# An encoder trunk on one core: attention units spread through the mixer, the Fourier parts reordered, and the second product of a gate block moved

## The chip, the core and the metric

One core of a Trainium2 chip runs the whole program: two layers of a bidirectional encoder on 512 tokens of width 1024, all in 32-bit floats. The metric is the time of one execution on the device in microseconds (us), as the median of several runs. Besides that there is one execution taken by the hardware profiler, with a record of every instruction; all rows of the profile are from it.

The engines have short names in the rows: PE is TensorE (matmuls), DVE is VectorE, ACT is ScalarE, POOL is GpSimd, SP is SyncE, which here only issues DMAs.

## The reference

Each of the two layers does three steps, and a norm stands at the end:

```python
x = x + 0.5 * swiglu(rms_norm(x, ffn1_norm[l]), ffn1_w_in[l], ffn1_w_out[l])
x = x + mixer(rms_norm(x, mix_norm[l]), mix_w_in[l], mix_gate_bias[l], na_rpb[l],
              na_w_out[l], f_w_out[l], mix_w_o[l])
x = x + 0.5 * swiglu(rms_norm(x, ffn2_norm[l]), ffn2_w_in[l], ffn2_w_out[l])
```

The change touches only the mixer. From one projection of the normed input it takes q, k, v (8 heads of 64), u (512 columns) and two gate inputs (1024 columns each):

```python
y_na = neighbourhood_attention(q.reshape(shp), k.reshape(shp), v.reshape(shp), rpb) @ w_na_out
y_f = fourier_mix(uf) @ w_f_out
g_na = jax.nn.sigmoid(ga + gate_bias[0])
g_f = jax.nn.sigmoid(gf + gate_bias[1])
return (g_na * y_na + g_f * y_f) @ w_o
```

The attention is local: on a grid of 8 x 64 tokens each query sees 8 x 16 keys, with a learned bias per head and offset, and a softmax over them. The Fourier part is the real part of a two-dimensional DFT over positions and over the 128 channels of each of four groups.

## The kernel before, in words

**Split matmuls.** Every 32-bit operand that goes through a matmul is cut into a high half, which the fast matmul type holds exactly, and a low half, the rest. A product is three matmuls: high x high, high x low, low x high. For weights this is `Item.prep` (line 192): ACT makes `whi` (L206; L201 with a minus sign; L186 in `prep_high`), DVE makes `wlo` (L209, L202, L190). Where the weight is a sum or difference, DVE first adds a second block in place (L178). There are three buffers each for `whi` and `wlo`.

**The stream of weights.** The weights come as blocks ("granules") of 128 x 1024, 512 KB, in one list that `stage_items` writes out in the order of use. `Stream.fetch` issues loads on SP's queue up to `FETCH` = 8 items ahead of the last prepared one, but never beyond the current stage; `Stream.enter` opens the next stage. Some blocks are sums that a DMA makes: POOL issues a load that adds to what is there (L164, and L211, which turns the weight of product 6 into that of product 3). `Stream.next(ahead)` prepares the item that is due and `ahead` (mostly 2) more.

**Products by Strassen.** A large product of 2 x 2 blocks is made from seven smaller ones, numbered 1 to 7 (`product`, lines 551 to 577). Each takes two granules and, with both halves of 256 tokens, 24 matmuls. The weights of the seven come from the quadrants a, b, c, d: product 1 takes -a, 2 takes b, 4 takes d (loaded anew), 5 takes d - c, 6 takes that plus a, 7 takes c - a and 3 takes product 6's weight with b added by POOL (signs lie in the sums). So b is a plain load, while product 5's weight is a load and a DMA that adds onto it. `ORDER` = (1, 5, 2, 6, 7, 3, 4) is the order in the gates.

**The mixer before the change** (`stage_mixer`), in order:

1. `proj_UV`: u and v by seven products, with projections of q and k (`proj_T`, one head pair each) between them.
2. Fourier transform over positions (`four_pos`, `rotated`) and over channels (`four_ch`, `four_mid`, `four_high`, `four_ends`).
3. Attention in eight units of `Probs` (two per head pair): scores on PE (`att_scores`, L1397), maxes with the bias on DVE (L1413), exps on ACT (L1422), reciprocals of the sums (L1425), scaling on ACT (L1430), transposes on PE (`transposed`, L1438), a copy by ACT (`kept`, L1448), then per head pair the product with v (`att_pv`, L1463) and the split of its result (`att_split`, L1473 and L1474). The units went in pairs: 0 and 1, 2 and 3, and so on, each pair's steps close together.
4. The Fourier output's product with its weights, in an even part (`part_f` with m = 0, plus the ends) and an odd part (m = 1) per half i of the output columns and per half t of the tokens. `f_copy` takes the even part, `f_both` makes their sum and difference, `f_last` adds single rows by short DMAs of POOL (L1671, L1673), `f_turn` puts the sums in their mirrored places by eight DMAs of SP (L1661) for each i. Order before: even 0, odd 0, even 1, odd 1, strewn between the attention units.
5. `swap_pools(0)`: the mixer's own pool of tiles is closed, its memory becomes nine buffers for weights, and the gates' stage opens. This stands behind the transposes of units 6 and 7.
6. `fill`: the attention output's product with its weights (L337 to L339), left half of the columns.
7. Two gate blocks (`gate_block`) of seven products each, whose results go through tanh and multiply the two outputs (`arg`, `with_f`, `with_n`). In block 1 the outputs of block 0 are turned over by transposing DMAs (`apart`, L374, and `joined_words`, L387). Then the rest of the attention output's product and the product with w_o.

**What sets the order.** From the start of `proj_UV` to the last `f_turn`, PE, DVE and ACT run in the order in which the program is written (the `manual_schedule` blocks). The queues of SP and POOL aren't written out by hand: a planner puts their DMAs in place, in about the program's order, and a queue runs strictly in its order, so that a DMA that waits holds those behind it. The gate blocks themselves are planned for PE and DVE too, with parts of ACT in written order.

Of the kernel before, what the change touches and what calls it, by code (L numbers as in the profile page):

```python
# [23 lines left out]
TB = T // P  # L24
# [8 lines left out]
ORDER = (1, 5, 2, 6, 7, 3, 4)  # L33
FETCH = 8
# [63 lines left out]
def encoder_kernel(  # L98
# [117 lines left out]
    def stage_items():  # L216
# [52 lines left out]
        for l in range(L):  # L269
# [16 lines left out]
            for i in range(2):  # L286
                strassen(s, lambda q: "g" + q, i, two, ORDER, True)
# [834 lines left out]
    def stage_mixer(l, norm, nxt):  # L1122
# [74 lines left out]
        vt, vch = [None] * TB, {}  # L1197
# [18 lines left out]
        def proj_UV():  # L1216
# [30 lines left out]
            step(6)  # L1247
            q0 = proj_T(DH**-0.5)
# [32 lines left out]
            product(pa, acts[7], K4, False, again=True, ahead=0)  # L1281
            ws.depth = FETCH
# [83 lines left out]
        o, q, k, bms = [], {}, {}, {}  # L1366
# [136 lines left out]
        def gate_block(i, bias, acts, after):  # L1503
# [37 lines left out]
            for m in ORDER:  # L1541
# [52 lines left out]
        yf = []  # L1594
# [80 lines left out]
        first_f = []  # L1675
        with tc.manual_schedule(engines={mybir.EngineType.DVE, mybir.EngineType.Activation}):
            with tc.manual_schedule(engines={mybir.EngineType.PE}):
                u, k1, pa, sb, acts4 = proj_UV()
                fp = [four_pos(0), four_pos(1)]
                bias_for(0)  # L1680
                k1 = k1()
                ws.prep(ws.pos + 2)
                bt = [rotated(fp[0]), rotated(fp[1])]
                less(pa, sb)
                k[1] = k1()
                ends_load()
                q2 = proj_T(DH**-0.5)
                q2 = q2()
                p0, p1 = [Probs(i, att_scores(i)) for i in range(2)]
                p0.maxes(0)  # L1690
                p0.maxes(1)
                ws.prep(ws.pos + 3)
                p0.exps(0)
                p1.maxes(0)
                p0.inverse(0)
                p0.exps(1)
                p1.maxes(1)
                p0.inverse(1)
                p1.exps(0)
                product(pa, acts4, K4, False, again=True, ahead=0)  # L1700
                q[2] = q2()
                for c in range(2):
                    value(c, pa[c])
                f0 = four_ch(bt)
                bias_for(1)
                p1.exps(1)
                fp = [four_pos(2), four_pos(3)]
                p1.inverse(0)
                p1.inverse(1)
                k2 = proj_T(None, 0)  # L1710
                for c in range(2):
                    value(2 + c, sb[:, c, :])
# [3 lines left out]
                p0.scaled(0)  # L1716
                y0 = y0()
                p0.scaled(1)
                bt.append(rotated(fp[1]))
                p1.scaled(0)  # L1720
                p1.scaled(1)
                k2 = k2()
                ws.prep(ws.pos + 2)
                key_rows()
# [5 lines left out]
                q3 = proj_T(DH**-0.5, 0, hook=second)  # L1730
                y1 = four_high(fq[0], 1)
                ye = four_ends(fq[1])
                q3 = q3(False)
                yf += [y0, y1()]
                ye()
                ends_split()
                ts = transposed(p0.s) + transposed(p1.s)
                pt_ = {0: kept(ts[0:2]), 1: kept(ts[2:4])}
                q3 = q3()
                p2, p3 = [Probs(i, att_scores(i)) for i in (2, 3)]  # L1740
                k3 = proj_T(None, 0)
                p2.maxes(0)
                p2.maxes(1)
                ws.prep(ws.pos + 1)
                low = ws.prep_high()
                p2.exps(0)
                p2.exps(1)
                p2.inverse(0)
                p3.maxes(0)
                p2.inverse(1)  # L1750
                low()
                p2.scaled(0)
                p2.scaled(1)
                p3.exps(0)
                p3.maxes(1)
                k[2] = k2()
                p3.inverse(0)
                p3.exps(1)
                q[3] = q3()
                p3.inverse(1)  # L1760
                p3.scaled(0)
                p3.scaled(1)
                k3 = k3(False)
                bias_for(2)
                first_f.append(ws.next(0))
                raw = ws.items[ws.pos - 1].raw.t
                first_f.append(ws.next(0))
                pf = part_f(0, 0, first_f[0], 0)
                ts = transposed(p2.s)
                f_copy(0, 0, pf)  # L1770
                pf = part_f(0, 1, first_f[0], 0)
                pl = last_f(0, raw)
                pt_[2] = kept(ts)
                k3 = k3()
                ts = transposed(p3.s)
                f_copy(0, 1, pf)
                pt_[3] = kept(ts)
                f_last(0, pl)
                k[3] = k3()
                p4, p5 = [Probs(i, att_scores(i)) for i in (4, 5)]  # L1780
                po = [att_pv(0), att_pv(1)]
                p4.maxes(0)
                p4.maxes(1)
                ws.prep(ws.pos + 1)
                p4.exps(0)
                p5.maxes(0)
                p4.inverse(0)
                p4.exps(1)
                p5.maxes(1)
                p4.inverse(1)  # L1790
                p4.scaled(0)
                p4.scaled(1)
                bias_for(3)
                ws.enter(ws.stage + 1)
# [81 lines left out]
        for _ in fill(o, ns, 0, w):  # L1876
            pass
# [324 lines left out]
```

## Time and profile before

| | |
|---|---|
| median of 3 runs | 1876.02 us |
| the three runs | 1877.15, 1876.02, 1864.79 us |
| profiled execution, its own time | 1877.13 us |
| span of its instructions | 1875.3 us |
| mean granted clock of PE | 0.993 |
| PE busy | 1834.1 us, 98% |
| DVE busy | 1604.9 us, 86% |
| ACT busy | 1305.6 us, 70% |
| DMA | 405.87 MB, mean 216 GB/s |

A row of groups reads: line, engine, operation, out <- in by the program's names, shapes, count | busy us, mean ns of one | idle time just before them and what ended it. A row of a timeline reads: start us, length us, engine, line, operation, out <- in, count, and in brackets the idle time before it with what ended it. A row of waits reads: who <- whom: total us, times, longest. A row of stretches reads: from:to, length, then for each engine the busy time and the number of instructions, the granted clock (1.00 is full), the busy share of the DMA engines (it can come out a little over 1) and GB/s. Records of matmuls overlap, since they are pipelined, so the pace of a run of matmuls is read from their starts. "SPq" is SP's queue issuing a DMA.

### The profile page before, as it was taken

How to read it: one execution, taken by the hardware profiler on the slowest of the kernel's cores; microseconds unless marked ns; L12 is line 12 of the kernel's file. 1: busy time of each engine (PE TensorE's matmuls, PEld its weight loads, DVE VectorE, ACT ScalarE, POOL GpSimd, SP SyncE). 2: the span in 40 equal slices, each digit the busy share in tenths (PEclk: the TensorE clock that was granted, in tenths of full speed). 3: DMA queues.
4: the chain of work that ended last, by engine and by line, in shares of the span. 5: the costliest groups of instructions: out<-in, count | busy, mean ns of one | idle time of the engine just before them, and what ended most of it. 6: DMA issues, size and time to landing. Idle time of an engine off the chain costs nothing.

```text
span 1875.3 us, 24536 instructions
## 1 busy us (share of the span) xinstructions
PE 1834.1 (98%) x8778; PEld 1513.5 (81%) x8778; DVE 1604.9 (86%) x1938; ACT 1305.6 (70%) x1775; POOL 187.5 (10%) x231
## 2 busy tenths in 40 slices
PE   9999999999899999999999999999998899999998
PEld 7888888887678888888888888877877688888886
DVE  7878899877789988889998879988778699888899
ACT  6777876657576767786666778665675677677865
POOL 0001010100101011001011000101011100110010
PEclk9999999999999999999999999999999899999999
DMA  9898798863987689879878987978549977998795
GB/s 297 225 237 219 194 266 279 207 180 111 271 219 180 158 236 238 215 208 275 248 188 225 220 219 205 285 264 174 157 148 246 202 181 174 224 229 217 202 286 149
DMA packets 206770, 405.87 MB, mean 216 GB/s; under 512 B 109116, under 2 KB 109276, under 8 KB 206648
## 3 DMA queue, kind: packets, MB, share of 16 engines
q1 hardware_dynamic: 176536, 302.61, 51.0%
q0 software_dynamic: 29680, 101.14, 30.1%
q8 instruction: 69, 1.13, 0.2%
q10 hardware_dynamic: 432, 0.55, 0.1%
q14 instruction: 53, 0.43, 0.1%
HBM read 372.76 MB, written 2.11 MB: 200 GB/s over the span
## 4 chain that ended last, share of the span: by engine, by line
PE 88%; DMA 5%; DVE 4%; ACT 1%; issue 1%; SPq 0%; POOL 0%; DVEq 0%; ACTq 0%; POOLq 0%
PE A L532 9%; PE A L535 9%; PE A L533 9%; PE o L535 6%; PE o L532 6%; PE o L533 6%; PE B L533 5%; PE B L535 5%; PE B L532 5%; DMA raw<-in_wst_dram 3%; PE ps L337 3%; PE ps L338 3%; PE ps L339 3%; PE C L532 2%; PE C L533 2%; PE C L535 2%
## 5 line engine op out<-in xcount | busy, mean ns | idle before, releaser
L209 DVE TENSOR_TENSOR wlo<-raw,whi 128x1024 fp32r<-128x1024 f32 (+1 forms) x532 | 629.8, 1195 | 189.2 <-ACT whi L206 186.7
L206 ACT ACTIVATE whi<-raw 128x1024 fp32r<-128x1024 f32 (+1 forms) x532 | 544.0, 1034 | 292.2 <-DMA raw<-in_wst_dram 59.4
L164 POOL DMA_DIRECT2D raw<-in_wst_dram x170 | 148.8, 895 | 1216.8 <-DMA raw<-in_wst_dram 527.6
L178 DVE TENSOR_TENSOR raw<-raw,raw 128x1024 f32<-128x1024 f32 (+1 forms) x152 | 181.6, 1195 | 2.0
L532 PE MATMUL A<-whi,xh 128*128 128x512 f32 x400 | 155.9, 390 | 2.7 <-ACT whi L201 2.7
L533 PE MATMUL A<-whi,xl 128*128 128x512 f32 x400 | 155.7, 389 | 0.0
L387 ACT ACTIVATE at<-zt 128x1024 uint16<-128x1024 uint16 (+2 forms) x96 | 110.4, 1168 | 12.3 <-DMA zt<-zs 12.1
L201 ACT ACTIVATE whi<-raw 128x1024 fp32r<-128x1024 f32 (+1 forms) x83 | 85.6, 1036 | 45.4 <-PE A L533 13.6
L535 PE MATMUL A<-wlo,xh 128*128 128x512 f32 x400 | 115.0, 389 | 0.0
L202 DVE SCALAR_TENSOR_TENSOR wlo<-raw,whi 128x1024 fp32r<-128x1024 f32 (+1 forms) x83 | 98.6, 1195 | 16.3 <-ACT whi L201 16.3
L532 PEld LDWEIGHTS A<-whi,xh 128*128 128x128 f32 x400 | 75.1, 188 | 18.9 <-ACT whi L201 3.5
L535 PEld LDWEIGHTS A<-wlo,xh 128*128 128x128 f32 x400 | 75.1, 188 | 15.6
L533 PEld LDWEIGHTS A<-whi,xl 128*128 128x128 f32 x400 | 75.1, 188 | 15.4
L533 PE MATMUL C<-whi,xl 128*128 128x512 f32 x208 | 81.0, 389 | 0.0
L533 PE MATMUL B<-whi,xl 128*128 128x512 f32 x208 | 81.0, 389 | 0.0
L532 PE MATMUL B<-whi,xh 128*128 128x512 f32 x208 | 81.0, 389 | 0.0
L532 PE MATMUL C<-whi,xh 128*128 128x512 f32 x208 | 81.0, 389 | 0.0
L368 ACT ACTIVATE zs<-th 128x1024 uint16<-128x1024 uint16 x80 | 79.5, 1042 | 0.9 <-DVE th L792 0.9
L785 ACT ACTIVATE th<-sn,rh 128x512 f32<-128x512 f32 x80 | 54.9, 716 | 32.7 <-DVE sn L622 31.8
L617 ACT ACTIVATE sn<-A 128x512 f32<-128x512 f32 x104 | 58.6, 586 | 25.2 <-PE A L535 25.2
L535 PE MATMUL C<-wlo,xh 128*128 128x512 f32 x208 | 60.1, 390 | 0.0
L535 PE MATMUL B<-wlo,xh 128*128 128x512 f32 x208 | 59.8, 389 | 0.0
(446 smaller groups left out, 4643.3 us busy)
## 6 DMA issues: line engine op xcount, KB each, us to landing
raw<-in_wst_dram SPq DMA_DIRECT2D x472, 512.0 KB
raw<-in_wst_dram POOLq DMA_DIRECT2D x180, 512.0 KB, 8.1
bm<-in_bias_dram SPq DMA_DIRECT2D x16, 512.0 KB
raw<-in_wst_dram SPq DMA_DIRECT2D x30, 256.0 KB
vs<-v SPq DMA_DIRECT2D x24, 128.0 KB
x<-in_xin_dram SPq DMA_DIRECT2D x4, 512.0 KB
raw<-in_wst_dram POOLq DMA_DIRECT2D x8, 256.0 KB, 7.8
dft<-in_dft_dram POOLq DMA_DIRECT2D x8, 256.0 KB, 6.7
```

The costliest lines, as they stand in the source:

```text
L164: G.dma_start(out=self.t, in_=wst[GRAN_AT[self.plus]][:, 0 : self.n], accum_op=ALU.add)
L178: V.tensor_tensor(self.raw.t, self.raw.t, self.add.t, self.op)
L201: S.activation(hi, t, AF.Copy, scale=-1.0)
L202: self.last = V.scalar_tensor_tensor(lo, t, -1.0, hi.bitcast(F32), ALU.mult, ALU.subtract)
L206: S.activation(hi[:, cs], t[:, cs], AF.Copy)
L209: self.last = V.tensor_tensor(lo[:, cs], t[:, cs], hi[:, cs].bitcast(F32), ALU.subtract)
L368: S.activation(s[:, h], words[:, h], AF.Copy)
L387: S.activation(to[:, w], t[:, w], AF.Copy)
L532: PE.matmul(ps, lh, rh, start=start, stop=False, skip_group_check=again)
L533: PE.matmul(ps, ll, rh, start=False, stop=False, skip_group_check=again)
L535: PE.matmul(ps, lh, rl, start=False, stop=stop, skip_group_check=again)
L617: S.activation(t[:, b, :], ps[b], AF.Copy)
```

## The change

Five things, all of them in the order of work; no operation is added or taken away.

- **Scores spread.** `proj_UV` now issues the scores of unit 0 behind the projection of q1 and those of unit 1 behind product 3, with their maxes, exps, reciprocals and part of the scalings among the rest of the u/v work. Units 2 to 7 follow one at a time, each with its own transposes, instead of in pairs. The bias of the first head pair is loaded from within `proj_UV`, the others earlier than before.
- **Even parts first.** The two even Fourier parts of both i (with their weights, which now come first in the stream) are done between units 4 and 7, with `f_last` for both at once. The odd parts come last: i = 0 ahead of the transposes of unit 7, i = 1 behind them.
- **The swap and the row turns.** `swap_pools(0)` stands behind the transposes of unit 7, now the last. Behind it come the odd parts of i = 1, the last `att_pv`, and both `f_turn`, which before stood ahead of it (i = 0) and behind it (i = 1). The attention output's weights are fetched later (`ws.enter` behind the split of `po[2]`).
- **Order at the hand-over.** `fill` is inside the written order for DVE and ACT now, with the first gate weight prepared ahead of it, and the sums of activations t1 to t3 are placed around it.
- **Gates.** Block 0 takes its products in the order `FIRST` = (1, 2, 5, 6, 7, 3, 4), and the stream lists its weights so.

```diff
+FIRST = (1, 2, 5, 6, 7, 3, 4)
...
-            for i in range(2):
-                t1, t2 = (s, "f", 2 * i), (s, "f", 2 * i + 1)
+            halves = [((s, "f", 2 * i), (s, "f", 2 * i + 1)) for i in range(2)]
+            for t1, t2 in halves:
                 add(Raw(t1, plus=t2))
+            for t1, t2 in halves:
                 add(Raw(t1), Raw(t2), op=ALU.subtract)
...
-                strassen(s, lambda q: "g" + q, i, two, ORDER, True)
+                strassen(s, lambda q: "g" + q, i, two, ORDER if i else FIRST, True)
...
             k[0] = k0()
+            p.append(Probs(0, att_scores(0)))
             product(pb, acts[3], K4, False, again=True)
             q1 = q1()
+            p[0].maxes(0)
+            p[0].maxes(1)
+            p[0].exps(0)
+            p[0].exps(1)
+            p.append(Probs(1, att_scores(1)))
             less(pb, s2)
+            p[0].inverse(0)
+            p[0].inverse(1)
...
             constants()
+            p[1].maxes(0)
+            p[1].maxes(1)
+            p[0].scaled(0)
+            p[0].scaled(1)
...
             product(pa, acts[7], K4, False, again=True, ahead=0)
+            ws.prep(ws.pos + 1)
+            p[1].exps(0)
+            p[1].exps(1)
```

The end of the attention, as it is after the change:

```python
                p.append(Probs(7, att_scores(7)))
                p[6].inverse(0)
                p[6].inverse(1)
                f_w.append(ws.next(0))
                raws.append(ws.items[ws.pos - 1].raw.t)
                pf = [part_f(0, t, f_w[1], 1) for t in range(2)]
                pl = [last_f(i, raws[i]) for i in range(2)]
                p[7].maxes(0)
                p[7].maxes(1)
                p[6].scaled(0)
                p[6].scaled(1)
                p[7].exps(0)
                p[7].exps(1)
                f_copy(1, 0, pf[0])
                f_copy(1, 1, pf[1])
                for i in range(2):
                    f_last(i, pl[i])
                po.append(att_pv(2))
                ts = transposed(p[6].s)
                p[7].inverse(0)
                p[7].inverse(1)
                p[7].scaled(0)
                p[7].scaled(1)
                first = minus(B[0, 0], B[0, 1], "t1")
                next(first)
                next(first)
                pt_[6] = kept(ts)
                att_split(po[2])
                ws.enter(ws.stage + 1)
                ws.prep(ws.pos + 2)
                f_w.append(ws.next(0))
                f_both(0, 0, part_f(1, 0, f_w[2]))
                f_both(0, 1, part_f(1, 1, f_w[2]))
                ts = transposed(p[7].s)
                swap_pools(0)
                pt_[7] = kept(ts)
                f_w.append(ws.next(0))
                ws.prep(ws.pos + 2)
                pf = [part_f(1, t, f_w[3]) for t in range(2)]
                po.append(att_pv(3))
                f_both(1, 0, pf[0])
                att_split(po[3])
                f_both(1, 1, pf[1])
                f_turn(0)
                f_turn(1)
                t12, _ = next(first)
                third = minus(B[0, 1], B[1, 1], "t3")
```

And the hand-over to the gates:

```diff
+            w = [ws.next(0), ws.next(0)]
+            ws.prep(ws.pos + 1)
             h1 = high(t12, "t1")
-            ws.prep(ws.pos + 3)
-            third = minus(B[0, 1], B[1, 1], "t3")
-            next(third)
             acts[5] = low(h1, t12, "t1")
+            for _ in fill(o, ns, 0, w):
+                pass
             for z in B[1, 1]:
                 V.tensor_tensor(t12, t12, z, ALU.add)
             h2 = high(t12, "t2")
             next(third)
             acts[6] = low(h2, t12, "t2")
-            w = [ws.next(), ws.next()]
-        for _ in fill(o, ns, 0, w):
-            pass
+            next(third)
...
-        ga0 = gate_block(0, bias, acts, {1: third_parts, 6: fourth})
+        ga0 = gate_block(0, bias, acts, {1: third_parts, 6: fourth}, FIRST)
```

More of the change, by code (lines that the diff above doesn't have):

```diff
@@ L1501, in fill, with gate_block @@
                 yield
-        def gate_block(i, bias, acts, after):
+        def gate_block(i, bias, acts, after, order=ORDER):
             r = norm.r
@@ L1540, in gate_block @@
             ga = [None, None]
-            for m in ORDER:
+            for m in order:
                 if m == 1:
@@ L1763, in stage_mixer @@
+                p[5].exps(0)
+                p[5].exps(1)
                 k3 = k3(False)
[L1764 to L1773, printed above, removed]
@@ L1805, in stage_mixer @@
-                ts = transposed(p4.s) + transposed(p5.s)
-                pt_[4] = kept(ts[0:2])
-                pt_[5] = kept(ts[2:4])
-                second_f = [ws.next(0)]
-                raw = ws.items[ws.pos - 1].raw.t
-                p6, p7 = [Probs(i, att_scores(i)) for i in (6, 7)]
-                po = att_pv(2)
-                p6.maxes(0)
-                ws.prep(ws.pos + 1)
-                p6.maxes(1)
-                p6.exps(0)
-                p7.maxes(0)
-                p6.inverse(0)
@@ L1818, in stage_mixer @@
-                p6.exps(1)
-                p7.maxes(1)
-                p6.inverse(1)
-                p6.scaled(0)
-                p6.scaled(1)
-                pf = [part_f(0, t, second_f[0], 1) for t in range(2)]
-                second_f.append(ws.next(0))
-                pl = last_f(1, raw)
-                f_turn(0)
-                p7.exps(0)
-                p7.exps(1)
+                bias_for(3)
+                f_w = [ws.next(0)]
+                raws = [ws.items[ws.pos - 1].raw.t]
```

174 lines of the change are left out of this document (82 added, 92 removed).

## The prediction

> **What bounds the kernel now.** First the page: TensorE (PE) is busy nearly the whole span, so a gain has to come from its pauses.
>
> ```profile
> span 1875.3 us, 24536 instructions
> PE 1834.1 (98%) x8778; PEld 1513.5 (81%) x8778; DVE 1604.9 (86%) x1938; ACT 1305.6 (70%) x1775; POOL 187.5 (10%) x231
> ```
>
> Then the busy time by stretches (us, PE, PEld, DVE, ACT, POOL, granted clock, DMA share, GB/s), cut where the mixer's parts begin and end; first layer 0, then layer 1.
>
> ```profile
> 367.60:405.00 37.40, 37.40 (x207) 31.20 (x206) 29.16 (x58) 21.46 (x44) 5.00 (x8) 1.00 0.77 229
> 405.00:460.00 55.00, 53.60 (x418) 42.41 (x417) 40.89 (x113) 45.09 (x119) 4.08 (x6) 1.00 0.26 78
> ...
> 470.28:486.75 16.47, 12.08 (x49) 8.70 (x48) 10.49 (x10) 9.34 (x13) 2.30 (x3) 1.00 1.02 290
> 486.75:497.85 11.10, 11.10 (x49) 8.93 (x48) 11.10 (x12) 6.22 (x8) 1.85 (x3) 1.00 0.89 252
> 497.85:509.52 11.67, 7.34 (x26) 5.59 (x24) 7.79 (x9) 4.82 (x6) 1.72 (x2) 0.85 1.05 274
> 509.52:520.40 10.88, 10.88 (x50) 9.01 (x48) 10.88 (x14) 6.27 (x7) 1.73 (x2) 1.00 0.81 207
> 520.40:561.40 41.00, 38.41 (x170) 31.45 (x168) 33.55 (x36) 30.73 (x34) 3.48 (x4) 1.00 0.85 216
> ```
>
> ```profile
> 1334.00:1389.00 55.00, 53.60 (x419) 42.41 (x418) 40.90 (x113) 45.08 (x119) 4.07 (x6) 1.00 0.27 77
> ...
> 1399.43:1415.89 16.46, 12.90 (x50) 9.79 (x48) 9.55 (x9) 9.31 (x13) 1.72 (x2) 0.90 1.02 285
> ...
> 1427.03:1436.81 9.78, 7.36 (x26) 5.57 (x25) 7.99 (x9) 4.83 (x6) 1.72 (x2) 0.83 1.04 269
> ...
> 1447.71:1496.32 48.61, 40.80 (x169) 33.23 (x168) 33.50 (x36) 30.82 (x34) 3.81 (x5) 0.89 0.89 192
> ```
>
> Gate block 0 begins at 470.28. Products 3 and 4 (509.52 to 520.40) run without a pause, so a product costs 10.88 / 2 = 5.44 and one of its 24 matmuls 0.227. Against that, products 1 and 5 lose 16.47 - 10.88 = 5.59 (layer 1: 5.58), product 7 loses 11.67 - 5.44 = 6.23 (layer 1: 9.78 - 5.44 = 4.34). That is **21.74** in all. Block 1 loses 41.00 - 38.08 = 2.92 and 10.53 more. Attention (405 to 460, 1334 to 1389) pauses 1.40 a layer, while the DMA engines stand at 0.26 and 0.27; in the gates they are full.
>
> ```profile
> PE A L532 <- ACT sn L617: 4.3, 1, 4.3
> PE B L532 <- ACT whi L206: 2.5, 2, 1.8
> PE A L532 <- ACT whi L201: 1.8, 1, 1.8
> ```
>
> ```profile
> PE A L532 <- ACT sn L617: 2.4, 1, 2.4
> ```
>
> These are PE's waits in block 0 of layer 0, and the one of product 7 in layer 1. The first is product 7: PE waits for the snapshot of product 6, which ACT holds back behind a weight that hasn't landed:
>
> ```profile
> 478.63 1.06 ACT L206 ACTIVATE whi<-raw 128x1024 fp32r<-128x1024 f32 x1 [1.77 <-DMA raw<-in_wst_dram]
> ...
> 496.69 0.60 ACT L617 ACTIVATE sn<-A 128x512 f32<-128x512 f32 x1 [1.20 <-PE A L535]
> 502.11 1.06 ACT L206 ACTIVATE whi<-raw 128x1024 fp32r<-128x1024 f32 x1 [4.82 <-DMA raw<-in_wst_dram]
> 503.07 0.58 ACT L617 ACTIVATE sn<-A 128x512 f32<-128x512 f32 x1
> ```
>
> The row at 478.63 is the first half of d for product 5, which came 8.4 after the gates' start. The weight at 502.11 is product 3's: quadrant d, to which POOL adds b in place (L211) once product 6's low half is made. POOL's issues, block 0 and block 1, and the page's median landing:
>
> ```profile
> 492.98 0.86 POOL L211 DMA_DIRECT2D raw<-in_wst_dram  x1 [6.09 <-DVE wlo L209]
> ...
> 535.54 0.87 POOL L211 DMA_DIRECT2D raw<-in_wst_dram  x1 [17.75 <-DVE wlo L209]
> ```
>
> ```profile
> raw<-in_wst_dram POOLq DMA_DIRECT2D x180, 512.0 KB, 8.1
> ```
>
> And SP's queue, which says why the gates' weights start late: their first six loads stand behind the row turns L1661, which wait for the last odd part.
>
> ```profile
> 322.52 0.80 SPq L1372 DMA_DIRECT2D bm<-in_bias_dram  x2
> ...
> 402.67 7.61 SPq L1208 DMA_DIRECT2D vs<-v  x12
> ...
> 457.13 4.24 SPq L1661 DMA_DIRECT2D fs<-gs  x5
> 461.49 3.56 SPq L154 DMA_DIRECT2D raw<-in_wst_dram  x6
> ...
> 1386.31 4.24 SPq L1661 DMA_DIRECT2D fs<-gs  x5
> 1390.66 2.96 SPq L154 DMA_DIRECT2D raw<-in_wst_dram  x6
> ```
>
> **The change, part by part.** No matmul, activation or DVE operation is added or removed; all is order. Prices:
>
> ```profile
> L209 DVE TENSOR_TENSOR wlo<-raw,whi 128x1024 fp32r<-128x1024 f32 x504 | 611.4, 1223 | 187.6 <-ACT whi L206 185.1 <-PE o L533 1.4 <-PE A L535 0.8
> ...
> L1413 DVE CUSTOM_DVE_ANT_0 s<-ps,bm 128x256 f32<-128x256 f32 x64 | 23.7, 418 | 0.7 <-PE ps L1397 0.7
> ```
>
> ```profile
> L206 ACT ACTIVATE whi<-raw 128x1024 fp32r<-128x1024 f32 x504 | 526.8, 1056 | 286.5 <-DMA raw<-in_wst_dram 57.6 <-DVE raw L178 57.0 <-PE A L533 54.6
> ...
> L1422 ACT ACTIVATE s<-s,nmx 128x256 f32<-128x256 f32 x64 | 31.6, 498 | 1.3 <-DVE nmx L1413 1.3
> L1430 ACT ACTIVATE s<-s,rs 128x256 f32<-128x256 f32 x64 | 27.0, 501 | 4.3 <-DVE rs L1425 4.2
> ```
>
> ```profile
> L1438 PE MATMUL ps<-ident,s 128*128 128x128 f32 x128 | 16.6, 275 | 1.8 <-ACT s L1430 1.8
> L1463 PE MATMUL ps<-p,vs 128*64 128x128 f32 x256 | 15.3, 275 | 0.0
> ...
> L1642 PE MATMUL ps<-raw,nyq 128*32 128x512 f32 x16 | 4.2, 605 | 0.0
> ```
>
> (1) *Scores spread.* A unit is 12 short score matmuls, four maxes (23.7 / 64 x 4 = 1.5; 1.7 by the mean) on DVE, four exps (2.0) and four scalings (1.7) on ACT. Units 0 and 1 go into 367.6 to 405, where DVE is busy 29.16 and ACT 21.46 of 37.40: 3.4 and 7.4 us fit. The tightest place there is the first Fourier product, which needs the low halves of u:
>
> ```profile
> 379.46 2.50 DVE L1192 TENSOR_TENSOR u<-ue,u 128x512 fp32r<-128x512 f32 x4
> ```
>
> They end at 381.96, PE comes at 367.60 + 3 x 5.44 = 383.92: 2.0 to spare. The eight maxes (3.0 to 3.4) and short reciprocals push them back by 3.4 to 4, the two scores push PE back by some 1.8 with their changes of kind, and the last halves are wanted one to two us into the product. So I count nothing; if that cover is gone, it costs up to 2 a layer. The 1.40 of pauses stand between pairs of units (transposes behind scalings); with one unit at a time each scaling has at least 5 us of PE's other work ahead of it, so 2.8 are gained for both layers (bound: 0). Two more changes of matmul kind per layer cost some 0.2 each: 0.8 (an estimate, 0 to 0.8).
>
> (2) *Even parts first, odd behind.* The last odd parts now need their weights prepared behind unit 7's softmax. From the scores of unit 7 on, PE has two even parts (16 matmuls, 3.7), two last rows (4.2 / 4 each, 2.1), a P·V product (15.3 / 8 = 1.9), two sets of transposes (16.6 / 16 each, 2.1) and two odd parts (2.7): 12.5 us before it wants them. ACT and DVE have to finish unit 6's exps (2.0, and some 2 until they begin), then copies of transposes (1.0), scalings (1.7), exps (2.0), two differences (2.4), the split of a head's output (0.6), the high half (1.0) and the low half (1.2): about 14. So a new wait of 0 to 1.8, for which I take 1.1 a layer: 2.2.
>
> (3) *SP and POOL.* The biases move up (before, SP issued them at 322.52, long ahead of use), the twelve row copies L1208 move behind the values: some 7.6 us from about 407, wanted at about 428: nothing. All 16 row turns move behind the gates' first loads. From the last transposes (where the pool is swapped) PE has 12 matmuls of odd parts (2.7), a P·V product (1.9) and 48 of the fill (10.9) before the gates: 15.5 us. The loads began 470.28 - 461.49 = 8.8 ahead; now up to 15.5. Both short accumulate chains of the last Fourier rows now come just ahead of the swap on POOL; the pool's memory or POOL may hold loads until about where they start now. That is the lower bound of the head start: none.
>
> (4) *Product 2 second.* Quadrant b is a plain load; d needs a load and then an accumulate (8.1). Now d comes 8.4 after the gates' start (478.63) and is wanted at 5.44; after the change it is wanted at 10.9, with b's two loads ahead of it. Even without a head start nearly all of product 5's wait is covered; with it, all. I leave 0.5 a layer for the second half of product 1's weights (0 to 1.8, today's wait L201, since ACT still makes t2's high half about there): 1.0.
>
> (5) *Product 7.* POOL's L211 goes out 0.57 after product 6 begins (497.85 - 5.44 = 492.41). In block 1 product 6 begins at 520.40 + 16.32 = 536.72, so it goes out 1.2 before; without the squeeze that the late d makes, ACT and DVE can do it as soon as product 2's buffers are free, up to 2.9 before. The snapshot is wanted 5.44 + 0.9 = 6.3 after the start; landing 8.1 (page) to 9.1 (492.98 to 502.11) and a high half of 1.0: left over 0 to 2.6. I take 1.3 a layer, 2.6, and no slow clock behind it (0.85 and 0.83 in the two stretches of product 7 now).
>
> [...]
>
> **Sum**: 21.74 - 1.0 - 2.6 + 2.8 - 2.2 - 0.8 = 17.9 off the profiled execution's 1877.13, which is 1.1 above the median of 1876.02: **1858**. Bounds: 21.74 + 2.8 = 24.5 to 21.74 - 3.6 - 5.2 + 2.8 - 3.6 - 0.8 = 11.3, so 1852 to 1865.
>
> **Rivals.** (A) *Block 1's wait goes as well.* In block 1 ACT waits for a transposing DMA:
>
> ```profile
> 1476.52 1.34 ACT L387 ACTIVATE mq<-zt 128x1024 uint16<-128x1024 uint16 x1 [7.61 <-DMA zt<-zs]
> ```
>
> If layer 1 behaves like layer 0, 48.61 becomes 41.00, 7.6 less: **1850**. For it: one of three runs shown is 11 shorter, and earlier weights leave the transposes freer. Against it: the steps around it aren't changed.
>
> (B) *The gates are bound by bytes.* Block 0 moved 290 x 16.47 + 252 x 11.10 + 274 x 11.67 + 207 x 10.88, 13.0 MB; at 290 GB/s that is 44.9 us, not 38.1. Without a head start layer 0 wins 50.12 - 44.9 = 5.2 and layer 1, whose block 0 takes 1447.71 - 1399.43 = 48.28, wins 3.4: **1867**. With 6.7 of head start it just fits. [...]
>
> (C) *It doesn't do what it says*: swap and loads stay where they are, and only product 5's wait shrinks, about 4 a layer: **1868**.
>
> (D) *Slower: the written order blocks.* ACT, DVE and PE run strictly in it, and now a maxes or exps stands ahead of the next weights' split at 16 places. If each holds PE by its four maxes (1.7), that is 27 against 18 gained: **1885**. It decides from 1.1 us a place. Against it: DVE has 8 and ACT 16 us free in the stretch that takes units 0 and 1.
>
> **How the numbers follow.** Forecast 0.50, A 0.20, B 0.17, C 0.05, D 0.08. A measurement of this kernel tells about 1% from no change, here below 1857.3. The forecast's own range lies on both sides of that, a little less than half below (0.24); with nearly all of A, faster 0.43. Slower is D less its small cases, 0.07; the rest, 0.50, is within 1%. The range from 1847 (A with some of the forecast's upside) to 1874 leaves out D and the tails.
>
> **What would show it.** Right: block 0 at 38 to 41 us in both layers, product 5 third and without a wait, six gate loads issued 12 us or more ahead of the first gate product, clock 1.00 in product 7, attention with pauses of at most 2 us. Wrong: waits of PE for whi or wlo of the odd parts or for s at more than two places of 1 us; a DMA share still near 1.0 with PE waiting in product 7 or 3; gate start later than now relative to the u/v product's start.

## The result and the profile after

| | before | after |
|---|---|---|
| median | 1873.95 us (11 runs, 1864.79 to 1877.15) | 1861.78 us (11 runs, 1857.66 to 1869.91) |
| profiled execution | 1877.13 us | 1860.03 us |
| span of its instructions | 1875.3 us | 1858.3 us |

The ratio after to before is **0.9943, 95% interval 0.9924 to 0.9961**: 0.6% faster, 12.2 us by the medians. The forecast of 1858 is 3.8 low. That it came so near is in part luck: its largest term, block 0's losses, gave 5.8 where it was to give 18.1, and the profiled execution of before lies 3.2 above the median of its eleven runs.

The page of the kernel after, first its span and engines. PE's busy time is 4.6 lower with the same 8778 instructions.

```profile
span 1858.3 us, 24537 instructions
PE 1829.5 (98%) x8778; PEld 1514.2 (81%) x8778; DVE 1604.3 (86%) x1938; ACT 1306.1 (70%) x1775; POOL 187.7 (10%) x231
```

The stretches (length, then PE, PEld, DVE, ACT, POOL, clock, DMA share, GB/s): in layer 0 the attention, gate block 0, product 7 in it, block 1; then the same in layer 1.

```profile
405.00:460.00 55.00, 54.80 (x407) 43.31 (x406) 42.10 (x103) 41.53 (x107) 4.11 (x6) 1.00 0.34 98
...
468.67:515.67 47.00, 40.87 (x170) 33.08 (x168) 38.99 (x41) 24.14 (x28) 7.77 (x9) 0.93 1.00 270
...
490.43:504.79 14.36, 8.23 (x26) 6.23 (x25) 9.32 (x8) 7.30 (x9) 1.73 (x2) 0.76 1.06 269
...
515.67:556.71 41.04, 38.37 (x169) 31.46 (x168) 33.61 (x36) 30.73 (x34) 3.48 (x4) 1.00 0.89 217
```

```profile
1334.00:1389.00 55.00, 54.80 (x395) 42.89 (x395) 42.29 (x93) 39.61 (x94) 4.70 (x7) 1.00 0.34 110
...
1389.51:1435.11 45.60, 40.01 (x169) 32.27 (x168) 37.57 (x40) 23.88 (x28) 7.77 (x9) 0.96 1.00 278
...
1411.27:1424.23 12.96, 7.37 (x25) 5.42 (x25) 8.07 (x7) 7.16 (x9) 1.73 (x2) 0.87 1.05 257
...
1435.11:1480.64 45.53, 40.84 (x170) 33.25 (x168) 34.95 (x38) 30.95 (x35) 3.45 (x4) 0.93 0.88 206
```

In the attention PE pauses 0.20 of 55.00 where it paused 1.40. In block 0 the products 1, 2, 5 and 6 now run without a wait: from 468.67 to 490.43 are 21.76, four times 5.44. But product 7 takes 14.36 where it took 11.67, and 12.96 where it took 9.78. So block 0 is shorter by only 50.12 - 47.00 = 3.12 and 48.28 - 45.60 = 2.68. PE's waits over the whole span say the same: what is left is the snapshot, and the last odd parts hardly wait. Of the 19.1, product 7 of block 0 has 6.1 and 5.6, block 1 the rest. What product 7 loses beyond that (14.36 - 5.44 - 6.1 = 2.8 and 1.9) lies behind the wait, at a lower clock (0.76 and 0.87 in its stretches).

```profile
PE A L534 <- ACT sn L619: 19.1, 4, 6.1
...
PE ps L340 <- DVE wlo L210: 0.4, 2, 0.2
```

What holds the snapshot is seen on ACT (kernel after, its timeline), one row after the other on the engine:

```profile
491.06 1.06 ACT L207 ACTIVATE whi<-raw 128x1024 fp32r<-128x1024 f32 x1 [5.20 <-DMA raw<-in_wst_dram]
495.13 1.06 ACT L207 ACTIVATE whi<-raw 128x1024 fp32r<-128x1024 f32 x1 [3.02 <-DMA raw<-in_wst_dram]
496.10 0.58 ACT L619 ACTIVATE sn<-A 128x512 f32<-128x512 f32 x1
497.75 1.06 ACT L207 ACTIVATE whi<-raw 128x1024 fp32r<-128x1024 f32 x1 [1.07 <-DMA raw<-in_wst_dram]
498.71 0.58 ACT L619 ACTIVATE sn<-A 128x512 f32<-128x512 f32 x1
```

By ACT's order the first two are product 7's own weights, the two granules of c with a added by POOL; the third is product 3's, b added onto d. In the kernel before only the third came late (502.11 in the prediction's rows). POOL of the kernel after issued its additions onto c late, because it waited for c itself, and SP's queue says why:

```profile
482.29 0.86 POOL L165 DMA_DIRECT2D raw<-in_wst_dram  x1 [12.28 <-DMA raw<-in_wst_dram]
483.46 0.86 POOL L165 DMA_DIRECT2D raw<-in_wst_dram  x1 [0.31 <-DMA raw<-in_wst_dram]
```

```profile
453.64 2.79 SPq L1681 DMA_DIRECT2D fs<-gs  x3
456.53 3.86 SPq L155 DMA_DIRECT2D raw<-in_wst_dram  x6
460.43 13.61 SPq L1681 DMA_DIRECT2D fs<-gs  x13
474.14 0.83 SPq L1892 DMA_DIRECT2D gb<-in_gbias_dram  x2
475.02 3.05 SPq L155 DMA_DIRECT2D raw<-in_wst_dram  x4
```

The same place in SP's queue of the kernel before, behind the six loads of 461.49:

```profile
465.10 2.17 SPq L1661 DMA_DIRECT2D fs<-gs  x3
467.38 0.37 SPq L154 DMA_DIRECT2D raw<-in_wst_dram  x1
468.34 1.60 SPq L1882 DMA_DIRECT2D gb<-in_gbias_dram  x2
470.85 2.20 SPq L154 DMA_DIRECT2D raw<-in_wst_dram  x2
```

The six loads of a, b and d start 468.67 - 456.53 = 12.1 ahead of the gates (before 8.8). The two of c, next in the list, were issued at 467.38 and 470.85, 2.9 ahead of the gates' old start and 0.6 behind it. Now they start at 475.02, 6.4 behind the new one, with 13 row turns (3 before) and the biases ahead of them. In layer 1 it is the same: 1395.83 against a gates' start of 1389.51.

The span is 17.0 shorter: layer 0's gates start 1.61 earlier and its blocks take 3.12 less and 0.04 more; from there to layer 1's gates are 5.23 less, their blocks take 2.68 and 3.08 less, and 1.32 is behind them. The 5.23 and 3.08 can't be put down to the change. The same stretch between the gates takes 832.6 to 837.6 in the kernels below that have the spread scores, and zt_late, which runs the same instructions as the kernel after in the same order on every engine, takes 43.68 and 42.48 in block 1 where the kernel after takes 41.04 and 45.53: single executions differ by that much.

### The profile page after: what moved, and what is told of

The parts are those of the page before. It is cut to its first block, busy times and chain, and to the rows that moved or that the text cites. A ratio compares the mean times of both kernels' runs of the same rounds, so it can differ in the third digit from the quotient of the medians.

```text
span 1858.3 us, 24537 instructions
## 1 busy us (share of the span) xinstructions
PE 1829.5 (98%) x8778; PEld 1514.2 (81%) x8778; DVE 1604.3 (86%) x1938; ACT 1306.1 (70%) x1775; POOL 187.7 (10%) x231
## 3 DMA queue, kind: packets, MB, share of 16 engines
HBM read 372.76 MB, written 2.11 MB: 202 GB/s over the span
## 4 chain that ended last, share of the span: by engine, by line
PE 90%; DMA 4%; DVE 3%; ACT 2%; issue 1%; SPq 0%; ACTq 0%; DVEq 0%
PE A L534 10%; PE A L537 10%; PE A L535 10%; PE o L537 7%; PE o L534 7%; PE o L535 7%; PE B L534 5%; PE B L535 5%; PE B L537 5%; DMA raw<-in_wst_dram 2%; PE C L534 2%; PE C L535 2%; PE C L537 2%; PE ps L339 2%; PE ps L340 2%; PE ps L341 2%
```

## The experiments

Theory: product 7 is bound by its own weights, and these by their place in SP's order behind the row turns. First rival: by bytes, so that no order would help. Second: by ACT's order alone, the snapshot behind whatever weight is next. All ratios are to the kernel before, by its runs on the same chip.

| kernel | median us | ratio, 95% interval | block 0, layers 0 and 1 |
|---|---|---|---|
| after | 1861.78 | 0.9943 (0.9924 to 0.9961) | 47.00, 45.60 |
| c_first | 1849.12 | 0.9868 (0.9847 to 0.9889) | 43.73, 43.40 |
| no_copies | 1846.70 | 0.9866 (0.9843 to 0.9890) | 42.12, 41.81 |
| turn_early | 1864.39 | 0.9957 (0.9938 to 0.9976) | 49.06, 48.52 |
| late_swap | 1872.15 | 1.0005 (0.9986 to 1.0024) | 52.28, 50.91 |
| order_alone | 1866.11 | 0.9963 (0.9948 to 0.9978) | 49.64, 45.24 |
| old_order | 1860.14 | 0.9934 (0.9917 to 0.9952) | 49.17, 49.06 |
| snap_first | 1852.30 | 0.9890 (0.9868 to 0.9912) | - |
| zt_late | 1864.09 | 0.9949 (0.9931 to 0.9968) | 48.05, 46.13 |
| zt_behind | 1857.42 | 0.9922 (0.9900 to 0.9945) | 47.90, 46.82 |
| holds_block1 | 1848.29 | 0.9861 (0.9836 to 0.9887) | 45.25, 43.10 |
| holds_both | 1851.57 | 0.9883 (0.9855 to 0.9910) | - |

(Where block 0 has a dash, matmuls of block 1 run among its last ones.) Each block time is from one execution. The kernel after, zt_late and zt_behind share their block 0, and so do c_first and holds_block1; their times differ by up to 1.5, so less than that says nothing.

**c_first: c's loads ahead of the row turns.**

```diff
                 swap_pools(0)
+                ws.fetch(ws.prepped + 12)
                 pt_[7] = kept(ts)
```

> The kernel after, with one line: behind swap_pools(0) the stream fetches four items further, so that the two loads of c (product 7's weights in gate block 0) stand on SP's queue ahead of 13 row copies (13.61 us in the kernel after) and the two gate biases (0.83). Theory 1, SP's order: POOL adds a onto c some 14 us earlier than at 482.29 and 483.46, product 7 of block 0 takes 6 to 7 us in both layers in place of 14.36 and 12.96, block 0 takes 39 to 41, and the time is 1846 to 1852 us (1861.8 less 7.5 and 6). Theory 2, bytes: the transfers share the engines and come no earlier, product 7 still waits over 4 us, and the time stays within 4 us of 1862. Theory 3, a new wait: the row copies, some 1.7 us later, hold product 7's gate or the head start costs the attention its transfers; the time is over 1866.

1849.12 us: in theory 1's range. Eight loads now stand together, POOL adds a onto c 11.7 earlier, and PE no longer waits for c. SP's queue, POOL and stretches of this kernel (block 0 and its product 7, block 1):

```profile
456.43 4.24 SPq L155 DMA_DIRECT2D raw<-in_wst_dram  x8
460.71 19.79 SPq L1681 DMA_DIRECT2D fs<-gs  x13
```

```profile
470.60 0.86 POOL L165 DMA_DIRECT2D raw<-in_wst_dram  x1 [0.98 <-DMA raw<-in_wst_dram]
```

```profile
468.60:512.33 43.73, 39.97 (x169) 32.59 (x168) 40.44 (x41) 23.92 (x28) 7.25 (x9) 0.96 1.02 274
490.36:501.45 11.09, 7.33 (x25) 5.57 (x24) 8.17 (x8) 4.69 (x6) 1.21 (x2) 0.85 1.04 333
...
512.33:550.82 38.49, 38.38 (x170) 31.45 (x168) 31.32 (x34) 29.32 (x32) 3.99 (x5) 1.00 0.89 217
1427.08:1467.60 40.52, 38.41 (x169) 31.45 (x168) 32.92 (x36) 30.69 (x34) 3.45 (x4) 1.00 0.87 216
```

The split was not as expected, so that the time lies in theory 1's range is in part luck. Block 0 takes 43.73 and 43.40 (expected 39 to 41), 3.27 and 2.20 less than in the kernel after, because product 7 still takes 11.09 and 10.76: ACT now holds the snapshot behind product 3's weight alone. Block 1 gave 2.55 and 5.01 beside it, which was not expected. SP's rows show that the one line of the edit changed SP's order in block 1 too. Layer 1, the kernel after, then c_first:

```profile
1445.31 2.91 SPq L155 DMA_DIRECT2D raw<-in_wst_dram  x3
1449.25 4.18 SPq L376 DMA_TRANSPOSE zt<-zs  x1
```

```profile
1437.30 1.49 SPq L155 DMA_DIRECT2D raw<-in_wst_dram  x2
1440.07 3.34 SPq L376 DMA_TRANSPOSE zt<-zs  x1
```

Between the two transposing DMAs of block 1 stand two weight loads, in both layers, where the kernels before and after have three. The second one starts 12.99 behind the block's start and not 14.14, and ACT's copy of what it brings, which stands ahead of half of the snapshot, waits 0 and 1.91 (2.47 and 4.49 in the kernel after). The other kernels agree: block 1 of both layers takes 84.1 to 89.6 in sum in before, after, zt_late, turn_early and order_alone, which have three loads there, and 77.0 to 81.1 in c_first, no_copies, old_order and late_swap, which have two. No run changes this order alone.

Both blocks together win 5.8 and 7.2, in sum 13.0 against 12.7 by the medians. Of these, the 5.5 of block 0 are what c's place was worth there, by these executions. Copy by copy SP's part is small in the trace of the kernel after: 13 row copies keep SP for 13.61 us, 1.05 each, while the copies of 120 KB land 4.4 us after their issue (median). But here the 13 stand one behind the other ahead of c's loads.

**no_copies: the place or the bytes?** The row turns are left out and the rows that they fill set to zero, so that part of the Fourier output is not computed.

```diff
-            for t, s0, n, tb, d0 in FLIP:
+            for t, s0, n, tb, d0 in FLIP[:0]:
...
+            G.memset(fs[i, t][:, 1 - t, :], 0.0)
             V.tensor_copy(fs[i, t][:, t, :], ps)
```

> The kernel after without its row copies (16 transfers on SP in each layer): the second halves of the Fourier tiles are set to zero on GpSimd in their place, so that part of the computation is left out. Theory 1, the place on the queue is what costs: c's loads start at about 461, product 7 takes what it took in c_first (10 to 11.5 us), and the time is that of c_first, 1846 to 1852. Theory 2, the copies' bytes and packets slow the weights too: the additions onto d and c land earlier still, product 7 loses under 3 us, and the time is 1840 to 1845. Theory 3, neither: 1858 to 1864.

0.9866 against c_first's 0.9868: the place is what costs. Product 7 takes 9.46 and 9.17 (11.09 and 10.76 in c_first), which lies between the two theories. Whether the bytes have a share in these 1.6 a layer is not shown: in holds_block1, with the block 0 of c_first, it takes 12.60 and 10.46.

**turn_early: the same work ahead of c, cut otherwise.**

```diff
                 f_both(0, 1, part_f(1, 1, f_w[2]))
+                f_turn(0)
                 ts = transposed(p[7].s)
...
                 f_both(1, 1, pf[1])
-                f_turn(0)
                 f_turn(1)
```

> The kernel after with f_turn(0) in front of the change of pools: 8 of the 16 row copies stand on SP's queue ahead of the gates' six first loads and 8 behind them, in place of 3 and 13. Theory 1, the queue: the work on SP ahead of c's loads is the same, so product 7 of block 0 waits as in the kernel after, and the six loads, 4 to 5 us later, cost 0 to 4 us in products 1 and 5: 1861 to 1868. Theory 2: only copies behind the loads hold c; product 7 takes 5 us less in each layer: 1850 to 1856.

Theory 1. SP's queue and PE's waits in block 0 of layer 0:

```profile
453.26 6.32 SPq L1681 DMA_DIRECT2D fs<-gs  x8
459.68 3.21 SPq L155 DMA_DIRECT2D raw<-in_wst_dram  x6
462.99 9.79 SPq L1681 DMA_DIRECT2D fs<-gs  x8
```

```profile
PE A L534 <- ACT sn L619: 4.8, 2, 2.8
PE B L534 <- ACT whi L207: 2.7, 1, 2.7
```

c's loads start at 473.82, 1.2 earlier than in the kernel after; a, b and d 3.2 later. So product 5 waits again (2.7) and the snapshot less: the wait only moved.

**late_swap: all 16 row turns ahead of the gates' loads.**

```diff
                 ts = transposed(p[7].s)
-                swap_pools(0)
...
                 f_turn(1)
+                swap_pools(0)
```

> The kernel after with the change of pools behind both f_turn calls, so that all 16 row copies stand on SP's queue ahead of the gates' first weights (the head start of 12.1 us is undone, product order and the spread of the scores as in the kernel after). Theory 1, the queue: the six loads start 1 to 3 us behind the first gate product's old start, product 1 of block 0 waits 8 us or more, block 0 takes 52 to 58 us, and the time is 1874 to 1884. Theory 2: product 7's weights bind whatever stands ahead, the wait only changes its place, and the time is 1860 to 1868.

1872.15, just under the range of theory 1 and at the kernel before. Product 1 waits only 2.6 and 1.8, not 8. PE's longest wait in layer 1 is ahead of product 5:

```profile
PE B L534 <- ACT whi L207: 6.9, 1, 6.9
```

The loads begin at 466.59 and 1395.79, some 5 ahead of the first product (471.76 and 1400.26); product 5 waits for d's sum although product 2 stands ahead of it. The kernel before had 8.8 of head start. So this run has less of it than the kernel before, and doesn't show what spread scores and product order are worth by themselves.

**order_alone and old_order: the product order by itself, and all but it.** The first is the kernel before with `FIRST` in the stream and in block 0; the second the kernel after with `ORDER` in both.

> The kernel before with the product order alone: items and products of gate block 0 go 1, 2, 5, 6, 7, 3, 4; the attention and the Fourier stage are untouched. Theory 1: product 7's weights come at a time that the queues of SP and POOL set, whatever runs before it, so product 5's wait goes and product 7 waits by as much longer: block 0 still takes 48 to 50 us in both layers, and the time is 1871 to 1876 us. Theory 2, the prediction's steps taken one by one: product 2 covers d's addition (5.6 us in each layer) and product 7 loses what it lost before: 1862 to 1866.

> The kernel after with the old product order in gate block 0 (1, 5, 2, 6, 7, 3, 4); all the rest as in the kernel after. Theory 1 (product 7's weights come at a time that the queues set): product 5 waits 3 to 5 us for d's sum again in each layer, and product 7's wait is shorter by the same: block 0 takes 46 to 48 us, and the time is 1860 to 1864. Theory 2: the order is worth what the prediction gave to it, and the time is 1869 to 1873.

old_order came out as theory 1 had it by the time: without the new order the kernel after is no slower (0.9934 against 0.9943). Its blocks went otherwise: product 5 hardly waits (d has the head start), product 7 still does, and block 0 is 2.2 and 3.5 longer than in the kernel after while block 1 is 2.5 and 6.4 shorter. Block 1 has the order of c_first there, with two loads between the transposing DMAs, so the equal times don't show that the product order is worth nothing in block 0. order_alone gave 0.37%, which theory 1 missed and theory 2 nearly met, but not by theory 2's working: block 0 is 0.5 and 3.0 shorter than before, block 1 in this execution 1.5 and 3.8. The two parts, 0.37% and 0.66%, don't add up to what both give, 0.57%; with old_order's other order in block 1 they can't be expected to.

**snap_first: c_first, and product 3's weight behind the snapshot on ACT.**

```diff
                         s2 = snap(pa)
                         with_n(arg(s1, 0, 0), 0)
+                    if not i:
+                        ws.fetch(ws.prepped + ws.depth)
+                        with tc.issue_after(taken_last[0].ins):
+                            ws.prep(ws.prepped + 1)
```

> The kernel of c_first with one more hold: in gate block 0 the rounding of product 3's first weights on ScalarE (the copy that waits for b's addition onto d, 4.24 us in c_first in layer 0) may issue only behind both halves of product 6's snapshot. Theory 1, ScalarE's order: product 7 of block 0, 11.09 and 10.76 us in c_first, takes 5.4 to 6.5, product 3 at most 1.5 more than its 5.44, and the time is 1838 to 1845 us. Theory 2, the weights: product 3 needs that same sum of b and d, and waits for it itself, so what product 7 gains product 3 loses; the time stays within 3 us of 1849.

The wait in product 7 is gone, as theory 1 said, and the time isn't. The stretch of product 7 in layer 0 (5.52 in layer 1), then PE's waits in layer 0's blocks:

```profile
490.66:496.21 5.55, 5.55 (x26) 4.25 (x24) 2.28 (x3) 2.61 (x3) 0.00 (x0) 1.00 1.05 270
```

```profile
PE A L535 <- DVE xl L346: 1.8, 1, 1.8
PE ps L340 <- DVE wlo L210: 1.7, 1, 1.7
PE B L534 <- ACT whi L207: 0.8, 1, 0.8
```

Product 3 waits 0.8 for the weight, product 4 1.8 for the low half of its activations on DVE, and the product behind the gates 1.7 for its weights' low half. The time, 1852.30 (0.9890), is no better than that of c_first (0.9868). So ACT's order did hold the snapshot, but what it held is wanted right behind it.

**zt_late and zt_behind: block 1's snapshot.** In the kernel after it stands on ACT behind a copy that waits for the transposing DMA. The first moves the hook `channels(0)` from product 7 to product 3; the second holds the copies behind the snapshot.

```diff
-            joined_words(mq[0, j], turned[j])
+            with nullcontext() if j else tc.issue_after(taken_last[0].ins):
+                joined_words(mq[0, j], turned[j])
```

> The kernel after with one hook moved: in gate block 1, channels(0) runs behind product 3 and not behind product 7, so ScalarE reaches the snapshot of product 6 without standing first at a copy that waits for the transposing DMA. Theory 1: block 1's waits (2.7 us in layer 0, 4.7 in layer 1 with the snapshot as the releaser) fall under 1 us each, block 1 takes 38.5 to 40 us in layer 0, and the time is 1855 to 1859. Theory 2: the snapshot is held by late weights and not by that copy; the time stays at 1860 to 1864. Theory 3: the copy is now late for the first product behind the gates, which waits 2 us or more in its place: 1860 to 1866.

> The kernel after with one hold: in gate block 1 ScalarE's copies out of the transposing DMA's tile for the first half may issue only behind both halves of product 6's snapshot (moving the hook alone, as in zt_late, left ScalarE's order as it was). Theory 1: block 1's product 7 (8.40 and 12.89 us in the kernel after) takes 5.4 to 6.5, block 1 takes 38 to 39.5, and the time is 1851 to 1857. Theory 2: the snapshot was late for another reason, or the copies are now late for the products behind the gates; the time stays at 1859 to 1865.

zt_late didn't test it: the planned order of every engine stayed as it was, so its 0.9949 is a second measurement of the kernel after. In zt_behind block 1 took 38.98 in layer 0 (41.04), but in layer 1 the next in ACT's order took the place, and product 7 needs 13.02 (12.89 in the kernel after):

```profile
1463.21 1.06 ACT L207 ACTIVATE whi<-raw 128x1024 fp32r<-128x1024 f32 x1 [5.29 <-DMA raw<-in_wst_dram]
1464.17 0.58 ACT L619 ACTIVATE sn<-A 128x512 f32<-128x512 f32 x1
```

0.9922 is not told apart from 0.9943.

**holds_block1 and holds_both: c_first with both holds in block 1, then in both blocks.**

> The kernel of c_first, and in gate block 1 both what stood between the halves of product 6's snapshot in ScalarE's order may issue only behind the second half: the copies out of the transposing DMA's tile for the first half (as in zt_behind) and the rounding of product 3's first weights. Block 0 is that of c_first. Theory 1, ScalarE's order: product 7 of block 1 (5.85 and 7.88 us in c_first) takes 5.4 to 6 in both layers and nothing behind it waits longer: 1845 to 1849 us. Theory 2: the wait moves on, to product 3 or behind the gates: within 2 us of 1849.

> As holds_block1, with the hold of product 3's weights in block 0 too (as in snap_first). Theory 1: the gains of both holds stand beside each other, block 0 takes about 41.5 (its last product waits 1.8 for DVE's low part, as in snap_first) and block 1 about 38.5: 1843 to 1847. Theory 2: what a hold gains, DVE's chain for product 4 and the late sums of b and d give back: 1847 to 1853.

In holds_block1 block 1 runs all but without a pause in both layers, against 38.08 of plain matmuls:

```profile
514.34:552.51 38.17, 38.17 (x170) 31.46 (x168) 31.36 (x34) 29.24 (x32) 3.48 (x4) 1.00 0.87 215
1430.52:1468.68 38.16, 38.16 (x169) 31.46 (x168) 30.96 (x34) 28.84 (x32) 4.32 (x5) 1.00 0.91 224
```

The time, 0.9861, is that of c_first (0.9868) within the intervals, and block 0 was 1.5 longer in layer 0 of this execution. holds_both is theory 2: DVE's 1.8 ahead of product 4 and 1.9 behind the gates take back what the hold in block 0 gives. The fastest version is thus c_first, with or without the holds in block 1: 1.3 to 1.4% under before.

## Why the prediction was right, and where it wasn't

The forecast held in the chance that it put highest, a difference that can't be told from none by 1%, and the range holds the time. The sum did not hold by its terms. Of its own signs, the six loads 12 us ahead (12.1) and the short pauses of the attention came as hoped; block 0 of 47.00 and 45.60 (38 to 41), the clock of 0.76 and 0.87 in product 7 and a DMA share of 1.06 and 1.05 there with PE waiting did not.

- **Steps (1) and (2), the attention**, held as to the waits. The pauses went from 1.40 to 0.20 a layer (2.4 against 2.8). No new wait came for the scores, and the last odd weights cost 0.4 in all (the 0.20 that is left in each layer) where 2.2 was counted. But less time was won than that. These are the same 717 matmuls of layer 0, from product 2 of u and v to the gates, before and after:

```profile
356.72:470.28 113.56, 112.16 (x717) 91.09 (x716) 85.77 (x187) 73.78 (x169) 10.12 (x16) 1.00 0.55 165
```

```profile
355.69:468.67 112.98, 112.78 (x717) 90.92 (x716) 86.56 (x188) 76.27 (x173) 10.00 (x15) 1.00 0.55 167
```

  They take 0.58 less (0.52 in layer 1), since PE is busy 0.62 longer (0.68). So 1.1 was won in all, and 1.3 of the 2.4 went into longer busy time. The sum had 0.8 for costs of this sort, for changes of matmul kind, estimated at 0.2 each; around three such changes in the trace of before (at 428.05, 429.75 and 437.34) the starts lie 0.31 to 0.34 apart and not 0.23, some 0.1 each. What the 1.3 consist of was not tried.
- **Step (4), product 2 second**, held as a mechanism: products 1, 2 and 5 run without a wait, so the 11.2 that products 1 and 5 had lost are gone. But the head start does it as well: in old_order product 5 runs without a wait in its old place in layer 0, and in late_swap it waits in its new one. And without a head start the order won little of it: in order_alone products 1, 2 and 5 take 20.58 and 20.48 in sum, 22.13 and 22.16 before.
- **Step (3), SP and POOL**, had the six loads right (12.1 ahead; "up to 15.5") and failed in what it left out. It followed the row turns only as far as the loads in front of them. The next two in the list, c's, came to stand behind 13 of the turns. So the price of the moved turns is not nothing; putting c ahead of them takes 3.27 and 2.20 off block 0.
- **Step (5), product 7, is the step that failed.** It let product 7 wait only for b added onto d, 1.3 a layer. Its own weights came last: 14.36 - 5.44 = 8.9 and 12.96 - 5.44 = 7.5 were lost, 16.4 against 2.6. Of these, 11.7 are waits (6.1 and 5.6) and 4.7 the lower clock behind them, which the step put at nothing. That takes 13.8 of the 17.9 away. For idle time as short as 1.3 the traces bear the nothing out (1.75 or less in a stretch of the clock's grid was never followed by half clock, see the last section), but the waits were 6.1 and 5.6. The step's mechanism stands behind the true one: with c early it is what holds the snapshot (3.8 and 3.4 in c_first), nearly three times the 1.3 that was taken. In layer 0 of c_first b's addition was issued at 483.90 and ACT began on its result at 494.04, 10.1 later and not 8.1 to 9.1.

So the terms as they turned out give 5.8 from block 0 (3.12 and 2.68) and 1.1 from the attention: 6.9 in place of 17.9. The other 5.3 of the 12.2 lie where the prediction counted nothing, and the runs don't say how much of that is the change's; in block 1 of layer 1 (48.61 to 45.53) order_alone has 44.85, zt_late 42.48. That the forecast came near all the same is luck.

Rival B (bytes) does not explain product 7: c_first leaves out no transfer, and PE's wait for c is gone. Its 44.9 for block 0 decides nothing, since c_first moves only 274 x 43.73 = 12.0 MB in that stretch, the rest ahead of it; but the 290 GB/s that it took as the limit is passed in c_first's product 7 (333). Rival C's time is that of order_alone (1866.11 against 1868). Rival A's wait stayed in the kernel after (41.04, 45.53) and shrank in c_first (38.49, 40.52). Rival D did not come up.

## What to carry to other kernels

When transfers are moved on an in-order queue, list what then stands behind them, down to the last load of the stage, and not only what moves ahead. A load that a second DMA must still add to needs its place in the queue first, since its way to use is more than twice as long (6.0 us from issue to landing for a load, and 8.1 more for the addition, medians of the kernel after). Look at the order of the whole queue after an edit, too: one line ahead of block 0 changed what stands ahead of a transfer of block 1. And when one late operand is cured, look on the same engine for the next instruction in its order before counting the gain: here product 5's wait turned into c's, c's into b's sum, and that into DVE's low half.

## What was not expected of the hardware

After waits of like length PE's clock sometimes fell and sometimes didn't. A wait of 2.11 us in product 7 of no_copies (layer 0) cost 9.46 - 5.44 - 2.11 = 1.9 beyond itself, one of 2.11 in block 1 of c_first (layer 1) 0.3. In these traces it went by where the wait lies. In each trace the granted clock changes only at times that are whole multiples of 3.413 us apart: in the kernel before it falls at 503.90, 1408.43, 1432.32 and 1473.28, which are 265, 7 and 12 times 3.413 apart. Here are the stretch of that grid with the wait and the next one, in no_copies and in c_first (for c_first the wait runs from 1449.91 to 1452.02):

```profile
490.85:494.26 3.41, 1.30 (x7) 0.76 (x6) 3.38 (x4) 1.98 (x3) 0.21 (x1) 1.00 1.04 231
494.26:497.67 3.41, 3.41 (x10) 2.64 (x9) 2.70 (x3) 2.28 (x3) 0.00 (x0) 0.50 1.03 261
```

```profile
1448.31:1451.72 3.41, 1.59 (x8) 0.98 (x6) 0.05 (x1) 1.53 (x2) 0.00 (x0) 1.00 1.06 275
1451.72:1455.13 3.41, 3.11 (x13) 2.55 (x14) 1.23 (x1) 2.92 (x4) 0.00 (x0) 1.00 1.01 338
```

The first wait lies whole in one stretch, in which PE is idle for 2.11, and the next runs at half clock. The second is cut by a boundary into 1.82 and 0.30, and the clock stays. So it is in all thirteen traces, behind their first 20 us: a stretch at full clock with 1.96 us or more of idle time came up 42 times and was followed by half clock each time; one with 1.75 or less, 6863 times, and never was; of 12 between, 4 were. One stretch at half clock cost 1.9 beyond the wait (no_copies), two cost 2.8 (kernel after, layer 0). So here a wait of 2 to 3 us is best counted with up to 1.9 more, by where it falls on the grid; whether that is part of the scatter between executions was not tried.

Row turns on SP took 13.61 us for 13 in the kernel after and 19.79 with two more weight loads ahead of them. In 2.6 and 5.7 of these SP waited for weight loads to land. The rest, 11.0 and 14.1, differs too, and single issues took 0.59 to 1.59 in the kernel after (32 of them, median 0.79), so an issue of such a DMA wasn't a fixed price here.
